# Empty bytes between on-chip buffers, so that streamed activations and weights begin at chosen offsets modulo 256

## The chip, the cores and the metric

One core of a Trainium2 chip runs the whole program in one launch. The metric is device time in microseconds, the median of several executions. TensorE (PE) multiplies, VectorE (DVE), ScalarE (ACT) and GpSimd (POOL) work beside it, SyncE (SP) issues the loads of weights.

## The reference, cut to what matters

Two networks run one after the other on 256 tokens of 1,024 features. The first has four layers, each a mixer (RWKV-7 in layers 0 and 3, stick-breaking attention in 1, sparse attention "dsa" in 2) and a SwiGLU FFN with 2,816 inner columns. The second has two layers on two token streams (`x` and a context `ctx`, 256 tokens each): FFN, a mixing of four branches with differential attention, FFN; the last layer needs only keys and values of the context.

```
x = x + mixer_i(rms_norm(x));  x = x + swiglu(rms_norm(x), w_gu[i], w_down[i])     # i = 0..3
x = x + 0.5*g * swiglu(mod_norm(x), ffn1);  x = x + g' * mix(mod_norm(x), mod_norm(ctx))
x = x + 0.5*g'' * swiglu(mod_norm(x), ffn2)                                        # and ctx alike
```

All is fp32. Almost all of the work is `h @ w` with 256 tokens and weights that come from HBM once, so eleven FFNs stand at the centre.

## The kernel before, in words

**The product.** An fp32 product is made of three fp32r products (`mm3`, L183 to L187): each operand is split into a first part (hi, the value rounded to fp32r by ACT) and a second part (lo, the rest, by DVE), and hi·hi (L185), hi weight·lo activation (L186) and lo weight·hi activation (L187) are added up in PSUM. The stationary operand is a 128x128 piece of a weight's part; the moving operand is 128 features x 256 tokens of an activation's part, 256 columns. In the page's names `whi`, `wlo` are the weight's parts, `hh`, `hl` the parts of a normed activation, `acth`, `actl` those of the FFN's inner activation, `xm` those of rwkv's mixed inputs, `mgh`, `mgl` those of the merged branches.

**Weights.** `wload` (L168) loads 1,024 columns raw (SP's queue) and splits them in pieces of 512 columns: ACT writes `whi`, DVE writes `wlo`, 2,048 bytes per partition each, three buffers of each in the stream's pool. In six FFNs of the main stream (EXTRA: a1, a2, a3, 100, 200, 110; the label is which FFN, layer, stream) two more pairs lie in the FFN's own pool: of every five pieces three use the main buffers and two the extra ones.

**Two streams.** The main stream's pools grow from the low end of SBUF ("left"); a second stream F, with its own weight pool on the right side, does the context's FFNs and mixing beside the main stream wherever the scheduler finds room; its place in the order of work comes from priorities (`spread`, `on`). All engines run their instructions in order, each in its own queue; POOL's queue holds the norms' sums (`norm_scale`, L260), the roots (`rsqrt`, L247), some adds of the mixing and the masks.

**Where buffers lie.** A pool is a stack: tiles lie behind each other by size, in the order of their first use, and pools of a phase are opened and closed again over the same bytes. Sizes per partition: raw weights 4,096, a weight's part 2,048, `hh` or `hl` 8,192, `acth` or `actl` 8,192 (main: 8 blocks) or 5,120 (F: 5 blocks), scratch tiles 1,024: all multiples of 256, so that every buffer's start modulo 256 is that of its pool, set by the small tiles (`const`, tables, vectors) ahead of it. The constants end at 34,528, which is 224 modulo 256; the main weight pool follows (first parts from 46,816, second from 52,960), then the norm's scratch, and the phases' pools start at 62,240, which is 32. The right stack ends at 229,344 (224) and grows downward. That gives, modulo 256:

| where | activations begin at | weight parts, first / second |
|---|---|---|
| main FFNs, mixing, stick-breaking attention | 32 | 224 / 224 |
| the same six FFNs' extra buffers (two pieces in five) | 32 | 32 / 32 |
| dsa, projections | 96 | 224 / 224 |
| rwkv, mixed inputs `xm` | 160 | 224 / 224 |
| F's FFNs: `hh`, `hl` | 160 | 224 / 224 |
| F's FFNs: `acth`, `actl`; F's mixing | 224 | 224 / 224 |

Lines that the change touches: `Kern.__init__` (L71), `wload` (L168), `ffn` (L296), the pools of `rwkv` (L425), `dsa` (L825) and `mixing` (L1094).

Of the kernel before, what the change touches and what calls it, by code (L numbers as in the profile page):

```python
# [8 lines left out]
F32 = mybir.dt.float32  # L9
# [7 lines left out]
P = 128  # L17
# [32 lines left out]
class Packed:  # L50


    def __init__(self):
        self.at, self.n, self.parts = {}, 0, []

    def add(self, name, cols, make):
        self.at[name] = (self.n, cols)
        self.parts.append(make)
        self.n += cols


class Stream:


    def __init__(self, name, wp, side, raw, conv, parts, banks, order=None):
        self.name, self.wp, self.side, self.raw, self.conv, self.parts = name, wp, side, raw, conv, parts
        self.norm = None
        self.banks, self.order, self.turn, self.pace, self.later, self.more, self.count = banks, order, {}, None, None, None, 0


class Kern:  # L71
    def __init__(self, ctx, tc, a, cols):
        self.ctx, self.tc, self.nc, self.a, self.cols = ctx, tc, tc.nc, a, cols
        self.const = ctx.enter_context(tc.tile_pool(name="const", bufs=1))
        wm = ctx.enter_context(tc.tile_pool(name="wm", bufs=1, reuse_waits="tile"))
        self.main = Stream("m", wm, "left", raw=3, conv=3, parts=3,
                           banks={"mm": (0, 1, 2), "sc": (3, 4, 5), "r0": (0, 2, 4), "r1": (1, 3, 5)})
        self.S = self.main
        self.main.norm = ctx.enter_context(tc.tile_pool(name="nm", bufs=1, reuse_waits="tile"))
        self.pp = ctx.enter_context(tc.tile_pool(name="pp", bufs=1, space=PSUM))  # L80
        self.dram = ctx.enter_context(tc.tile_pool(name="dram", bufs=1, space=bass.MemoryType.DRAM))
        self.n = 0
        self.setup()

    def uid(self, s):
# [27 lines left out]
    def vec(self, name, i=0, n=1):  # L113
        at, _ = self.cols.at[name]
        return self.pv[:, at + i : at + i + n]

    def ps(self, tag="mm"):

        S = self.S
        b = S.banks[tag]  # L120
        i = S.turn.get(tag, 0)
        S.turn[tag] = i + 1
        b = b[i % len(b)]
        return self.pp.tile([P, 512], F32, name=self.uid(tag), tag=f"b{b}", bufs=1)
# [43 lines left out]
    def wload(self, src, n):  # L168

        nc, S = self.nc, self.S  # L170
        raw = self.raw(src, n)
        for c in range(0, n, CONV):
            e = min(CONV, n - c)
            self.paced()
            pool, bufs = S.more if S.more and S.count % (S.conv + S.more[1]) >= S.conv else (S.wp, S.conv)
            S.count += 1
            hi = pool.tile([P, CONV], F32R, name=self.uid("whi"), tag="whi", bufs=bufs)
            lo = pool.tile([P, CONV], F32R, name=self.uid("wlo"), tag="wlo", bufs=bufs)
            i = nc.scalar.activation(hi[:, :e], raw[:, c : c + e], AF.Copy)  # L179
            nc.vector.tensor_tensor(lo[:, :e], raw[:, c : c + e], hi[:, :e].bitcast(F32), op=ALU.subtract)  # L180
            yield c, e, hi, lo
# [114 lines left out]
    def ffn(self, pool, hs, w_gu, w_down, add, label):  # L296

        nc = self.nc
        S = self.S
        n = -(-KF // S.parts)  # L300
        S.more = (pool, EXTRA[label]) if label in EXTRA else None
        ends = [KF * (i + 1) // self.S.parts for i in range(self.S.parts)]
        for j0, j1 in zip([0] + ends, ends):
            acts = self.pair(pool, n, "act")[: j1 - j0]
            for j in range(j0, j1):
                p = self.ps()
                self.lin(p[:, :T], w_gu[j, 0], hs)
                self.lin(p[:, T:], w_gu[j, 1], hs)
                t = pool.tile([P, T], F32, name=self.uid("ft"), tag="ns", bufs=2)
                nc.scalar.activation(t, p[:, :T], AF.Tanh, scale=0.5)  # L310
                nc.vector.scalar_tensor_tensor(t, t, 1.0, p[:, :T], op0=ALU.add, op1=ALU.mult)  # L311
                nc.vector.scalar_tensor_tensor(t, t, 0.5, p[:, T:], op0=ALU.mult, op1=ALU.mult)  # L312
                self.split(pool, t, *acts[j - j0])
            for j in range(KD):
                p = self.ps()
                self.lin(p[:, :T], w_down[j][:, j0 * P : j1 * P], acts)
                add(j, p[:, :T])
        S.more = None

    def add_to(self, x):  # L320
# [16 lines left out]
    def rwkv_consts(self):  # L337
# [16 lines left out]
        self.lev = []  # L354
        with self.tc.tile_pool(name="lv", bufs=1, reuse_waits="tile") as A:
            row = A.tile([P, 1], I32, name="lrow")
            col = A.tile([P, HD], I32, name="lcol")
            for h in range(2):
# [3 lines left out]
            for sh in range(6):  # L362

                x = c.tile([P, HD], I32, name=f"lx{sh}")
                y = A.tile([P, HD], I32, name=f"ly{sh}", tag="ly")
                nc.vector.tensor_tensor(x, rowb, col, op=ALU.bitwise_xor)
# [36 lines left out]
    def rwkv(self, i, j, x, front, rear):  # L403

        nc, tc, a = self.nc, self.tc, self.a
        self.rwkv_consts()
        start = tc.cur_priority
        with tc.tile_pool(name=f"rw{j}", bufs=1, reuse_waits="tile") as R:
# [6 lines left out]
            with ExitStack() as es:  # L415
# [7 lines left out]
                    nc.vector.tensor_scalar(dd[:, k, 0:1], h[:, k, 0:1], -1.0, None, op0=ALU.mult)  # L423

                A = es.enter_context(tc.tile_pool(name=f"rwa{j}", bufs=1, reuse_waits="tile"))  # L425

                def plain(m):
                    xs = []
                    for k in range(KD):
                        xs.append(A.tile([P, T], F32, name=self.uid("xp"), tag="xp", bufs=10))  # L430
                        nc.vector.scalar_tensor_tensor(xs[k], dd[:, k], self.vec("rw_mix", (j * 6 + m) * KD + k), h[:, k],
                                                       op0=ALU.mult, op1=ALU.add)
                    return xs

                def first(out, src, xs, rank):
                    w = A.tile([P, KD * P], F32, name=self.uid("w1"), tag="w1", bufs=W1[j])
                    nc.sync.dma_start(w[:, : KD * rank], src)
                    for k, x in enumerate(xs):
                        nc.tensor.matmul(out, w[:, k * rank : (k + 1) * rank], x, start=k == 0, stop=k == KD - 1)
# [99 lines left out]
            with rear as go, tc.tile_pool(name=f"rwc{j}", bufs=1, reuse_waits="tile") as C, self.banks(**RB):  # L539
                ys, base, n, top = [], tc.cur_priority, 0, 0  # L540
                for f in range(KD):
# [3 lines left out]
                    n, top = n or tc.cur_priority - base, max(top, tc.cur_priority)  # L545
# [261 lines left out]
    def dsa(self, i, j, x):  # L807
        nc, tc, a = self.nc, self.tc, self.a
        V = nc.vector
        W3 = T + P  # L810
        with tc.tile_pool(name=f"ds{j}", bufs=1, reuse_waits="tile") as R:
# [11 lines left out]
            wi = R.tile([P, 2, 8], F32, name=self.uid("wi"))  # L823
            os = []
            with tc.tile_pool(name=f"dsa{j}", bufs=1, reuse_waits="tile") as A:  # L825
                hs = self.pair(A, KD, "h")
                self.normed(A, x, lambda f: self.vec("norm_mix", i * KD + f), hs)

                for f in range(5):
                    p = self.ps()  # L830
                    self.lin(p[:, :T], a["ds_w_idx"][j][f], hs)
                    s = A.tile([P, T], F32, name=self.uid("xs"), tag="xs", bufs=2)
# [3 lines left out]
                for tt in range(2):  # L836
                    p = self.ps()
                    for f in range(KD):
                        s = slice(f * 8, (f + 1) * 8)
# [30 lines left out]
                for dst, at, g in ((q, 0, gq), (k, KD, self.vec("ds_k_norm", j))):  # L870
                    for f in range(KD):
                        s = A.tile([P, T], F32, name=self.uid("qs"), tag="qs", bufs=2)
# [13 lines left out]
            with tc.tile_pool(name=f"dsc{j}", bufs=1, reuse_waits="tile") as C:  # L886
                for h in range(16):
# [9 lines left out]
                    s = C.tile([P, 2], F32, name=self.uid("s"), tag="s", bufs=3)  # L897
# [196 lines left out]
    def mixing(self, l, s, x, m, ahead=None):  # L1094

        nc, tc, a = self.nc, self.tc, self.a
# [3 lines left out]
        def sub(name):  # L1100
            return tc.tile_pool(name=f"{name}{l}{s}", bufs=1, reuse_waits="tile")
        with ExitStack() as ahead_pools, sub("mx") as M:
            hs = self.pair(M, KD, "h")
            oc, od, ob, oa = self.pair(M, 4, "oc"), self.pair(M, 2, "od"), self.pair(M, 2, "ob"), self.pair(M, 2, "oa")
            with sub("mn") as N:
                self.mod_norm(N, x, m, s, 1, hs)
            if ahead is not None:
# [379 lines left out]
```

## Time and profile before

| | |
|---|---|
| median of 3 executions | 3950.63 us (3942.87 to 3956.42) |
| the profiled execution | 3951.83 us, span 3950.1 us |
| granted TensorE clock, mean | 0.988 of 2.4 GHz |
| busy | PE 97%, DVE 68%, ACT 52%, POOL 7% |
| bytes read from HBM | 664.84 MB, 170 GB/s over the span |

The span runs from the first to the last instruction. Matmuls overlap in the records: one takes some 0.28 us from start to end, and the next starts when its own weights are in place and the array takes columns, so the spacing from start to start is what a matmul costs in a full stream. The timeline gives starts with two decimals, so spacings are taken over many matmuls. By stage (us in the span): rwkv of layer 0 to 560, its FFN a0 to 810, stick-breaking attention to 960, FFN a1 to 1180, dsa to 1490, FFN a2 to 1710, rwkv of layer 3 to 2250, FFN a3 to 2450, the second network's FFN 100 to 2670, mixing of layer 0 to 3080, FFN 200 to 3270, FFN 110 to 3480, mixing of layer 1 to 3765, FFN 210 to the end. F's FFNs and mixing run between 120 and 810, 920 and 1710, and 1710 and 3080, between the main stream's matmuls.

### The profile page before, as it was taken

The numbers are of one execution on the slowest core, as the hardware profiler recorded it, in microseconds if no ns is written. First come the engines' busy times: TensorE is split into PE (matmuls) and PEld (weight loads), VectorE is DVE, ScalarE is ACT, GpSimd is POOL, SyncE is SP. The second block draws the span as 40 slices with busy tenths as digits, with TensorE's granted clock in tenths as the row PEclk, the third lists the DMA queues.
The fourth block names the chain that finished last, engine by engine and source line by source line (L and its number), as shares of the span: only waits on it lengthen the run. The fifth ranks groups of instructions, "written<-read, shape, count | busy, mean of one in ns | idle before, by whom it ended". The sixth has DMA issues, their size and how long they took to land. (4 is left out here: it accounts for less than half of the span.)

```text
span 3950.1 us, 87281 instructions
## 1 busy us (share of the span) xinstructions
PE 3848.3 (97%) x34750; PEld 3600.8 (91%) x34750; DVE 2693.8 (68%) x5644; ACT 2041.9 (52%) x4137; POOL 295.0 (7%) x333
## 2 busy tenths in 40 slices
PE   7999999998999999999999999999999999999898
PEld 5787999986999999989778999999999999989898
DVE  6355667655777777677556767677966766668766
ACT  3333455577655555545333555555555555555454
POOL 0000000004301110000000100000001000000100
PEclk9999999998999999999999999999999999999999
DMA  7555355642664446646763565664455666644455
GB/s 264 177 168 174 96 170 183 202 148 86 183 183 126 154 155 195 190 128 189 256 227 109 164 187 179 197 186 149 145 181 179 185 190 209 187 146 133 135 180 162
DMA packets 199912, 676.80 MB, mean 171 GB/s; under 512 B 22416, under 2 KB 34960, under 8 KB 199376
## 3 DMA queue, kind: packets, MB, share of 16 engines
q1 hardware_dynamic: 196912, 668.66, 54.3%
q8 instruction: 273, 4.47, 0.5%
q10 hardware_dynamic: 2592, 2.56, 0.2%
q14 instruction: 135, 1.11, 0.1%
HBM read 664.84 MB, written 6.29 MB: 170 GB/s over the span
## 5 line engine op out<-in xcount | busy, mean ns | idle before, releaser
L180 DVE TENSOR_TENSOR wlo<-wraw,whi 128x512 fp32r<-128x512 f32 (+3 forms) x2256 | 1533.2, 687 | 854.0 <-ACT whi L179 810.8
L179 ACT ACTIVATE whi<-wraw 128x512 fp32r<-128x512 f32 (+3 forms) x2256 | 1370.9, 615 | 1349.8 <-PE mm L186 1117.3
L185 PE MATMUL mm<-hh,whi 128*128 128x256 f32 x5496 | 1542.0, 283 | 13.0 <-ACT hh L282 9.0
L187 PE MATMUL mm<-hh,wlo 128*128 128x256 f32 x5496 | 1543.1, 283 | 0.7 <-DVE wlo L180 0.7
L186 PE MATMUL mm<-hl,whi 128*128 128x256 f32 x5496 | 1541.3, 282 | 1.7 <-DVE hl L239 1.1
L185 PEld LDWEIGHTS mm<-hh,whi 128*128 128x128 f32 x5496 | 1039.2, 190 | 31.7 <-ACT hh L282 10.9
L186 PEld LDWEIGHTS mm<-hl,whi 128*128 128x128 f32 x5496 | 1039.6, 190 | 21.8 <-issue 13.4
L187 PEld LDWEIGHTS mm<-hh,wlo 128*128 128x128 f32 x5496 | 1038.4, 190 | 20.7 <-issue 13.9
L185 PE MATMUL mm<-acth,whi 128*128 128x256 f32 x1936 | 537.7, 282 | 3.5 <-DVE ft L312 1.2
L186 PE MATMUL mm<-actl,whi 128*128 128x256 f32 x1936 | 540.7, 282 | 0.4 <-DVE actl L239 0.4
L187 PE MATMUL mm<-acth,wlo 128*128 128x256 f32 x1936 | 538.6, 282 | 0.3 <-DVE wlo L180 0.3
L185 PEld LDWEIGHTS mm<-acth,whi 128*128 128x128 f32 x1936 | 363.2, 189 | 11.7 <-issue 5.3
L186 PEld LDWEIGHTS mm<-actl,whi 128*128 128x128 f32 x1936 | 365.0, 189 | 5.7 <-issue 4.1
L187 PEld LDWEIGHTS mm<-acth,wlo 128*128 128x128 f32 x1936 | 363.8, 189 | 5.5 <-issue 3.0
L260 POOL TENSOR_TENSOR nacc<-nacc,nsq 128x256 f32<-128x256 f32 x114 | 95.4, 838 | 1714.8 <-ACT nsq L259 1713.8
L247 POOL TENSOR_TENSOR ry<-ry,mhalf 128x4 f32<-128x4 f32 (+2 forms) x77 | 82.8, 1076 | 1477.7 <-DVE ry L246 1411.7
L238 ACT ACTIVATE acth<-ft 128x256 fp32r<-128x256 f32 x242 | 100.6, 416 | 55.9 <-DVE ft L312 48.9
L951 PE MATMUL mm<-wada,c 128*32 128x384 f32 x768 | 105.3, 522 | 11.3 <-DMA wada<-in_w_ada 11.3
L239 DVE TENSOR_TENSOR actl<-ft,acth 128x256 fp32r<-128x256 f32 x242 | 104.1, 430 | 4.0 <-ACT acth L238 3.2
L312 DVE SCALAR_TENSOR_TENSOR ft<-ft,mm 128x256 f32<-128x256 f32 x242 | 101.4, 419 | 6.4
L311 DVE SCALAR_TENSOR_TENSOR ft<-ft,mm 128x256 f32<-128x256 f32 x242 | 100.2, 414 | 0.0
L185 PE MATMUL mm<-xm,whi 128*128 128x256 f32 (+1 forms) x328 | 92.8, 287 | 1.9 <-ACT L L481 1.0
(433 smaller groups left out, 4838.4 us busy)
## 6 DMA issues: line engine op xcount, KB each, us to landing
wraw<-in_ffn_w_gu SPq DMA_DIRECT2D x484, 512.0 KB, 4.0
wada<-in_w_ada SPq DMA_DIRECT2D x96, 768.0 KB, 4.5
wraw<-in_w_g SPq DMA_DIRECT2D x96, 512.0 KB, 3.6
wraw<-in_ffn_w_down SPq DMA_DIRECT2D x64, 448.0 KB, 3.4
wraw<-in_ffn_w SPq DMA_DIRECT2D x64, 448.0 KB, 3.4
wraw<-in_rw_w_rkv SPq DMA_DIRECT2D x48, 512.0 KB, 3.9
wraw<-in_ffn_w SPq DMA_DIRECT2D x72, 256.0 KB, 2.8
wraw<-in_ffn_w_down SPq DMA_DIRECT2D x32, 512.0 KB, 3.6
```

What stands on the lines that cost most here:

```text
L179: i = nc.scalar.activation(hi[:, :e], raw[:, c : c + e], AF.Copy)
L180: nc.vector.tensor_tensor(lo[:, :e], raw[:, c : c + e], hi[:, :e].bitcast(F32), op=ALU.subtract)
L185: t.matmul(out, w[0], x[0], start=first, stop=False)
L186: t.matmul(out, w[0], x[1], start=False, stop=False)
L187: t.matmul(out, w[1], x[0], start=False, stop=last)
L238: self.nc.scalar.activation(hi, x, AF.Copy)
L239: self.nc.vector.tensor_tensor(lo, x, hi.bitcast(F32), op=ALU.subtract)
L247: nc.gpsimd.tensor_tensor(y, y, self.mhalf[:, :n], op=ALU.pow)
L260: (nc.vector if k in fast else nc.gpsimd).tensor_tensor(acc, acc, sq, op=ALU.add)
L311: nc.vector.scalar_tensor_tensor(t, t, 1.0, p[:, :T], op0=ALU.add, op1=ALU.mult)
L312: nc.vector.scalar_tensor_tensor(t, t, 0.5, p[:, T:], op0=ALU.mult, op1=ALU.mult)
L951: nc.tensor.matmul(p[32 * i : 32 * (i + 1), :384], c[:, k], raw[:, 384 * i : 384 * (i + 1)], start=k == 0, stop=k == KD - 1)
```

## The change

A method `gap` writes zeros on POOL to a tile that nothing reads, 64 to 192 bytes per partition, and so moves all that lies behind it. It is called at eight places: behind the main weight pool (128 bytes), between first and second parts in each weight pool at its first use (128: the main pool, F's pool, the extra buffers' pools), in the FFNs of EXTRA behind the first inner activations (64), in F's FFNs ahead of the inner activations (192) and at the end (64), at the head of the pools for rwkv's mixed inputs (128) and for dsa (192), and in F's mixing (64). No other instruction is touched.

```diff
+        self.n = 0
+        self.gap(ctx.enter_context(tc.tile_pool(name="sp", bufs=1)), 128)
         self.main.norm = ctx.enter_context(tc.tile_pool(name="nm", bufs=1, reuse_waits="tile"))
...
+    def gap(self, pool, n, tag="gap"):
+
+        self.nc.gpsimd.memset(pool.tile([P, n // 4], F32, name=self.uid(tag), tag=tag), 0.0)
...
             hi = pool.tile([P, CONV], F32R, name=self.uid("whi"), tag="whi", bufs=bufs)
+            if pool not in S.seen:
+                S.seen.append(pool)
+                self.gap(pool, 128, "mid")
             lo = pool.tile([P, CONV], F32R, name=self.uid("wlo"), tag="wlo", bufs=bufs)
...
+        if S.norm is None:
+            self.gap(pool, 192)
         for j0, j1 in zip([0] + ends, ends):
             acts = self.pair(pool, n, "act")[: j1 - j0]
+            if S.more and j0 == 0:
+                self.gap(pool, 64)
...
+        if S.norm is None:
+            self.gap(pool, 64, "end")
         S.more = None
...
                 A = es.enter_context(tc.tile_pool(name=f"rwa{j}", bufs=1, reuse_waits="tile"))
+                self.gap(A, 128)
...
             with tc.tile_pool(name=f"dsa{j}", bufs=1, reuse_waits="tile") as A:
+                self.gap(A, 192)
...
             oc, od, ob, oa = self.pair(M, 4, "oc"), self.pair(M, 2, "od"), self.pair(M, 2, "ob"), self.pair(M, 2, "oa")
+            if s:
+                self.gap(M, 64)
```

`S.norm` is set for the main stream only, so the two gaps that ask for it lie in F's FFNs.

## Rows read from the trace of the kernel before

**Rows 1.** Summary of the page: span, then busy time of each engine.

```profile
span 3950.1 us, 87281 instructions
...
PE 3848.3 (97%) x34750; PEld 3600.8 (91%) x34750; DVE 2693.8 (68%) x5644; ACT 2041.9 (52%) x4137; POOL 295.0 (7%) x333
```

**Rows 2.** The chain that ended last: shares of the span by line.

```profile
PE mm L187 6%; PE mm L186 6%; PE mm L185 6%; DVE wlo L180 0%; PE sc L213 0%; PE mm L231 0%; PE mm L233 0%; PE mm L232 0%; PE mm L1038 0%; DMA wraw<-in_w_qk 0%; DVE hl L283 0%; DVE mgl L1158 0%; DMA wraw<-in_w_br 0%; DVE gt L1153 0%; DVE nh L277 0%
```

**Rows 3.** Page's costliest groups: streamed matmuls on normed activations and inner ones.

```profile
L185 PE MATMUL mm<-hh,whi 128*128 128x256 f32 x5496 | 1542.0, 283 | 13.0 <-ACT hh L282 9.0
...
L185 PE MATMUL mm<-acth,whi 128*128 128x256 f32 x1936 | 537.7, 282 | 3.5 <-DVE ft L312 1.2
```

**Rows 4.** Timeline of PE, FFN 110 (EXTRA): start us, duration us, matmul.

```profile
3304.43 0.28 PE L185 MATMUL mm<-hh,whi 128*128 128x256 f32 x1
3304.55 0.28 PE L186 MATMUL mm<-hl,whi 128*128 128x256 f32 x1
...
3304.91 0.28 PE L186 MATMUL mm<-hl,whi 128*128 128x256 f32 x1
3305.02 0.28 PE L187 MATMUL mm<-hh,wlo 128*128 128x256 f32 x1
...
3308.87 0.28 PE L185 MATMUL mm<-hh,whi 128*128 128x256 f32 x1
3308.99 0.28 PE L186 MATMUL mm<-hl,whi 128*128 128x256 f32 x1
3309.11 0.28 PE L187 MATMUL mm<-hh,wlo 128*128 128x256 f32 x1
```

**Rows 5.** Timeline of PE, F's mixing, activation and weight at 224.

```profile
1379.26 0.28 PE L187 MATMUL mm<-hh,wlo 128*128 128x256 f32 x1
...
1380.94 0.28 PE L186 MATMUL mm<-hl,whi 128*128 128x256 f32 x1
```

**Rows 6.** Timeline of PE, dsa, activation at 96, weight at 224.

```profile
1255.60 0.27 PE L185 MATMUL mm<-hh,whi 128*128 128x256 f32 x1
...
1257.14 0.28 PE L186 MATMUL mm<-hl,whi 128*128 128x256 f32 x1
```

**Rows 7.** Timeline of PE, FFN 210 (no EXTRA), activation 32, weight 224.

```profile
3817.78 0.28 PE L185 MATMUL mm<-hh,whi 128*128 128x256 f32 x1
...
3838.04 0.28 PE L186 MATMUL mm<-hl,whi 128*128 128x256 f32 x1
```

**Rows 8.** Timeline of PE, rwkv 1 beside F's FFN, activations 160, weights 224.

```profile
1831.78 0.28 PE L185 MATMUL mm<-hh,whi 128*128 128x256 f32 x1
...
1833.59 0.28 PE L185 MATMUL mm<-hh,whi 128*128 128x256 f32 x1
1833.71 0.28 PE L186 MATMUL mm<-xm,whi 128*128 128x256 f32 x1
...
1835.97 0.28 PE L185 MATMUL mm<-hh,whi 128*128 128x256 f32 x1
```

**Rows 9.** Groups of PE in 3822 to 3844, then in 3305.9 to 3308.6.

```profile
L186 PE MATMUL mm<-hl,whi 128*128 128x256 f32 x63 | 17.6, 280 | 0.0
L187 PE MATMUL mm<-hh,wlo 128*128 128x256 f32 x63 | 17.6, 279 | 0.0
...
L187 PE MATMUL mm<-hh,wlo 128*128 128x256 f32 x9 | 2.5, 276 | 0.0
```

**Rows 10.** Windows: length, PE busy (count), weight loads, DVE, ACT, POOL, clock.

```profile
2260.00:2650.00 390.00, 390.00 (x3349) 389.91 (x3348) 267.58 (x500) 214.40 (x402) 9.83 (x12) 1.00 0.63 189
1510.00:1690.00 180.00, 180.00 (x1548) 180.00 (x1547) 119.50 (x223) 98.89 (x184) 7.18 (x8) 1.00 0.63 190
3090.00:3270.00 180.00, 180.00 (x1551) 180.00 (x1550) 123.44 (x227) 100.19 (x188) 4.76 (x6) 1.00 0.63 189
```

**Rows 11.** Window of the last mixing, same columns.

```profile
3480.00:3765.00 285.00, 273.05 (x2077) 255.70 (x2076) 215.05 (x439) 145.84 (x289) 20.47 (x18) 0.98 0.45 140
```

**Rows 12.** Groups of POOL over the span: count, busy us, mean ns, idle before.

```profile
L260 POOL TENSOR_TENSOR nacc<-nacc,nsq 128x256 f32<-128x256 f32 x114 | 95.4, 838 | 1714.8 <-ACT nsq L259 1713.8
L247 POOL TENSOR_TENSOR ry<-ry,mhalf 128x4 f32<-128x4 f32 (+2 forms) x77 | 82.8, 1076 | 1477.7 <-DVE ry L246 1411.7 <-ACT whi L179 66.0
...
L1479 POOL MEMSET const-float32-1.0<- 128x1 f32 x1 | 0.1, 99 | 0.0
```

More of the change, by code (lines that the diff above doesn't have):

```diff
@@ L66, in __init__ @@
         self.name, self.wp, self.side, self.raw, self.conv, self.parts = name, wp, side, raw, conv, parts
-        self.norm = None
+        self.norm, self.seen = None, []
         self.banks, self.order, self.turn, self.pace, self.later, self.more, self.count = banks, order, {}, None, None, None, 0
@@ L81, in __init__ @@
         self.dram = ctx.enter_context(tc.tile_pool(name="dram", bufs=1, space=bass.MemoryType.DRAM))
-        self.n = 0
         self.setup()
```

## The prediction

> **What bounds the kernel now.** I read the page's summary first: PE is busy for 97% of the span, nothing else for more than 68% [rows 1]. Then the chain of waits: the three lines of the streamed product, L185 to L187, carry 6.2% each, more than anything else on it [rows 2]. The engine therefore waits for little; the question is how fast its matmuls follow each other. The page's list of groups gives their number: 5,496 triples on the normed activations and 1,936 on the FFN's inner ones [rows 3], 22,296 matmuls; the code adds 3,048 of the same form (mixed inputs, attention outputs, merged branches), so 25,344 of the page's 34,750. One FFN is 22·2·8·3 + 22·8·3 = 1,584 of them.
>
> Then I laid the timeline beside the addresses of the section on the layout, and formed the distance of weight start minus activation start, modulo 256. Every matmul below streams 256 columns against a 128-column weight, at full granted clock, with no wait ahead of it:
>
> - Distance 0, both at 32: from 3304.43 to 3304.91 the starts lie 0.48/4 = 120 ns apart [rows 4]. Distance 0, both at 224: from 1379.26 to 1380.94 in 14 steps, 120.0 ns [rows 5].
> - Distance 128 (activation 96, weight 224): 1255.60 to 1257.14 in 13 steps, 118.5 ns [rows 6].
> - Distance 192 (activation 32, weight 224): two answers. Right behind the block at 120 ns in rows 4, from 3304.91 to 3308.87 in 35 steps, 113.1 ns (113.3 with the rounding of starts); in the last FFN, from 3817.78 to 3838.04 in 172 steps, 117.8 ns [rows 7].
> - Distance 64 (activation 160, weight 224): 1831.78 to 1835.97 in 37 steps, 113.2 ns [rows 8].
>
> So there are three paces, 113.3, 117.8 and 120 ns, and the form of the instruction is the same in all. Which one holds goes with the distance, and at 192 also with what ran before. The duration that the profile gives a matmul repeats it: 280 and 279 ns in the last FFN, 276 within the fast stretch of rows 4 [rows 9].
>
> **The change, part by part.** *Where buffers begin.* By adding up tile sizes: 128 bytes behind the main weight pool plus 128 between its parts shift all behind it by 256, so the main activations stay at 32, the first parts at 224, and the second parts go from 224 to 96. Distances in a triple become 192, 192, 64 (they were 192 three times). In the six FFNs with extra weight buffers (EXTRA: a1, a2, a3, 100, 200, 110) 64 + 128 bytes put the extra pair at 96 and 224 instead of 32 and 32: distances 64, 64, 192 instead of 0. The right stack grows downward, so 128 bytes between its parts put F's first parts at 96 and its second at 224; 192 + 64 in the FFN's pool and 64 in the mixing bring its activations from 160 and 224 to 32: distances 64, 64, 192 instead of 64 or 0. The gaps of 128 and 192 in the rwkv and dsa pools bring xm and hh from 160 and 96 to 32. No matmul at distance 0 or 128 is left.
>
> *What the present paces cost above 113.3 ns.* (1) Six FFNs with EXTRA, 9,504 matmuls: three windows in which PE ran little else give 390.00/3349 = 116.4, 180.00/1548 = 116.3 and 180.00/1551 = 116.1 ns [rows 10], say 116.3: two weights in five at 120, the rest near 113.3. 9,504 · 3.0 = 28 us. (2) The FFNs a0 and 210, without EXTRA, 3,168 matmuls at 117.8 [rows 7]: 3,168 · 4.5 = 14 us. (3) The other 12,672 (F's FFNs, mixings, projections) have no clean window; their blocks lie at 113.2, 117.8, 118.5 and 120 [rows 5 to 8], and I take the mean of those four, 117.4, less a little for the many at 113: 117.0, so 12,672 · 3.7 = 47 us (ends: 30 at 115.7, 57 at 117.8). Sum 89 us, with ends 72 and 99.
>
> *What of it comes out.* The new triple, 192, 192, 64, stands nowhere in the trace, so its pace is the unknown. Bounds by the nearest rows: 113.3 at one end, as both 192 and 64 run there [rows 4, 8]; at the other 117.8 [rows 7]. Lower than 113.3 I exclude, since no stretch of such matmuls shows it; 120 too, since it goes with distance 0 alone. I take 113.3: in rows 4 a stretch at 192 takes it up without any change in its own addresses and keeps it for 35 matmuls, up to the next block at 120; in rows 8 two streams interleave at 64 and hold it; the fast order survives in either, so a triple made of both has a pace that both sides keep, while each slow order belongs to one distance. A step from 192 to 64 in every triple is a small push out of that slow order, as the 120 block is in rows 4. But each wait on weights or a norm starts the sequence afresh, and a little of the saved time will be spent in waits: PE is less than fully busy in the attention stages, for instance 273.05 of 285 us [rows 11]. I count 80% of the sum: 71 us.
>
> *What it adds.* 25 small fills on POOL (2 at set-up, 12 in the six EXTRA pools, 7 for F's weights and FFNs, 4 in rwkv, dsa and mixing). The nearest rows are POOL's set-up fills of 99 ns [rows 12], together 2.5 us on an engine that is idle for 93%. Their price lies in POOL's queue: a fill waits until the memory it covers is free, and behind it stand the norm's sums (L260, 838 ns, 114 of them) and the roots (L247, 1,076 ns) [rows 12], for which the phase's first activations, and so its first matmuls, wait. Ends: 0, where POOL was idle anyway (L260 alone was preceded by 1,714 us of idleness), and one sum late per norm, 114/6 = 19 norms with six sums each on POOL, 19 · 0.84 = 16 us. I take 1, nearest to the idle end, since the norms' sums wait for ACT's squares. The same tiles in new places bring no other instruction, no transfer and no wait; the loads have no new trigger except PE's own faster release of weight buffers. If PE runs 2% faster, ACT and DVE must prepare weights 2% faster: DVE, at 68%, has the room, and would be late next only at phase starts.
>
> Sum: 3951.8 of the profiled execution (span 3950.1) − 71 + 1 = 3882. The profiled execution lies 1.2 us above the median shown, 3950.6, so I give 3882 against that median too.
>
> **The rivals.** (a) *Half the gain.* The fast order is taken up in the triples but lost at each break, or only a part of the stretches finds it. For it: the last FFN keeps 117.8 for 172 matmuls without slipping over [rows 7]. 89/2 = 44, less the waits: 3911.
>
> (b) *Slower: the slow order everywhere.* In the EXTRA FFNs the fast order follows a block at distance 0 [rows 4], while FFNs without such blocks run at 117.8 [rows 7]. If it is the 120 ns block that resets the order, the change removes what it was good for: 9,504 · (117.8 − 116.3) = +14 us; F's projections at 64 and the interleaved xm, some 4,150 matmuls with perhaps half at 113.2 [rows 8], +9; F's inner activations and mixing at 224, about 3,000 at 120 [rows 5], −7. Together +16: 3967. It decides where more than nine in ten of all matmuls run at 117.8: break-even with the mean of 116.8 is (117.8 − 116.8)/4.5 = 22% at the fast pace, and 0.3% slower is reached below 12%. Against it: rows 8, where distance 64 is fast without any such block.
>
> (c) *Nothing happens.* The pace hangs on another thing that goes with the stage (buffer turns, other engines' traffic), and addresses are only its companion: 3951. Against it: rows 4 switch from 120 to 113 and back within one stage and one code path, where only the weight buffer changes. The Trainium skill, "SBUF — State Buffer", section "Who interferes with whom", speaks for this rival: PE reads streamed operand and weights through two independent ports and waits on no one, so starts modulo 256 could not matter. By that rule the sum would be 0 to +2; the three paces in one stage speak against it.
>
> (d) *The roles are swapped.* In EXTRA pools and on F's side the first parts come to 96, not 224 as the change's words say. With all distances still 64 or 192 the time stays that of the forecast, or of (a) if only the order 192, 192, 64 is good.
>
> **How the numbers follow.** Forecast (with d) 0.62; (a) 0.13; (c) 0.10; (b) 0.15. No change of under 0.3%, about 12 us, can be told from none by a measurement of this kernel. Faster takes the forecast and (a), less a little of (a)'s edge, 0.74; same is (c) and that edge, 0.12; slower is 0.14. The range starts at 3951 − 89 = 3862, a little lower for the upper end of (3): 3858; it reaches to 3955, over (a) and half of (c), and leaves out (b) and little else.
>
> **What would show it.** Right: in the last FFN's timeline starts 113.3 ns apart instead of 117.8 and a mean duration of 276 instead of 280; the window 2260 to 2650 shorter by some 10 us for the same 3,349 matmuls; no block at 120 in an EXTRA FFN. Wrong: 117.8 in most windows means (b); blocks at 120 with distances of 64 or 192 mean (c); fast main stages and slow F stages mean that the roles in (d) count; a POOL fill ahead of L260 with PE idle at a phase start means that the fills cost more than 1 us.

## The result, and the profile after

The changed kernel takes 3890.82 us, the median of four runs (3878.99 to 3895.20), against 3953.53 us before beside it: a ratio of 0.9846 with an interval of 0.9830 to 0.9862, some 61 us less by the ratio. Two later sets gave 3894.58 and 3890.19 us. Two executions in them had a lower mean granted clock, 3944.53 us at 0.94 and 5353.16 us at 0.651: the first is in the second set's ratio below and widens its interval, the second is in no number here. The profiled execution, 3878.99 us, is the shortest of the four, so its trace shows a little more gain than the median.

The page's first lines, and of its costliest groups the two that answer to [rows 1, 3] (the lines have moved by eight, so L193 to L195 are the triple):

```profile
span 3877.2 us, 87308 instructions
...
PE 3773.0 (97%) x34750; PEld 3529.2 (91%) x34750; DVE 2687.3 (69%) x5644; ACT 2040.4 (53%) x4137; POOL 297.6 (8%) x358
...
L193 PE MATMUL mm<-hh,whi 128*128 128x256 f32 x5496 | 1529.3, 281 | 11.7 <-ACT hh L290 7.6
...
L193 PE MATMUL mm<-acth,whi 128*128 128x256 f32 x1936 | 532.0, 279 | 4.0 <-DVE xc L986 1.5
```

The bound is where it was: PE at 97% of a shorter span, the same number of matmuls. Taken matmul by matmul, the two traces have the very same order of all 34,750. The profiled gain of 73 us is spread over the whole span; at the same place in that order the new trace is 3 us ahead at 238 us of the old one, 20 at 1128, 35 at 1940, 49 at 2786, 65 at 3404 and 71 at 3850. It is the pace; PE's idle time, span less busy, is 104.2 us where it was 101.8. The timeline of the last FFN, the counterpart of [rows 7] (start, duration, engine, line, tile):

```profile
3800.02 0.28 PE L194 MATMUL mm<-hl,whi 128*128 128x256 f32 x1
3800.13 0.28 PE L195 MATMUL mm<-hh,wlo 128*128 128x256 f32 x1
...
3820.08 0.28 PE L194 MATMUL mm<-hl,whi 128*128 128x256 f32 x1
```

From 3800.02 to 3820.08 stand 177 steps, 113.3 ns each, where before every step took 117.8. But the same FFN has a stretch ahead of it that is not fast:

```profile
3732.89 0.28 PE L193 MATMUL mm<-acth,whi 128*128 128x256 f32 x1
3733.00 0.28 PE L194 MATMUL mm<-actl,whi 128*128 128x256 f32 x1
...
3752.50 0.28 PE L193 MATMUL mm<-hh,whi 128*128 128x256 f32 x1
```

19.61 us for 165 steps are 118.8 ns. That is a slow order of the new triple, and slower than the old one. It sets in behind a step of 181 ns at 3724.5, and the fast order is back at 3783.4 with no pause between them:

```profile
3724.51 0.34 PE L195 MATMUL mm<-acth,wlo 128*128 128x256 f32 x1
3724.69 0.28 PE L193 MATMUL mm<-acth,whi 128*128 128x256 f32 x1
...
3783.05 0.28 PE L195 MATMUL mm<-acth,wlo 128*128 128x256 f32 x1
3783.17 0.40 PE L193 MATMUL mm<-acth,whi 128*128 128x256 f32 x2
3783.41 0.28 PE L194 MATMUL mm<-actl,whi 128*128 128x256 f32 x1
```

It ends behind two L193 in a row (x2), a place where the program leaves the order of the triple; the three longest such stretches of the second trace end at places of this kind as well. Whether that is what ends them was not tried; another such place, at 3726.94, ends nothing.

By windows (length, PE busy and count, weight loads, DVE, ACT, POOL, granted clock, DMA share, GB/s), first two of before, an FFN with extra buffers and the last one:

```profile
3100.00:3200.00 100.00, 100.00 (x861) 100.00 (x860) 66.85 (x123) 53.48 (x99) 0.00 (x0) 1.00 0.63 187
3800.00:3860.00 60.00, 60.00 (x512) 60.00 (x511) 40.57 (x74) 31.80 (x60) 0.00 (x0) 1.00 0.62 186
```

and then of the changed kernel, the first line answering to [rows 10]:

```profile
2225.00:2595.00 370.00, 369.98 (x3262) 369.70 (x3261) 261.21 (x491) 209.51 (x394) 7.77 (x11) 1.00 0.63 194
3100.00:3200.00 100.00, 100.00 (x885) 100.00 (x884) 69.25 (x126) 56.58 (x106) 4.00 (x5) 1.00 0.64 195
3735.00:3785.00 50.00, 50.00 (x423) 50.00 (x422) 32.70 (x60) 26.96 (x51) 0.00 (x0) 1.00 0.60 184
3800.00:3860.00 60.00, 60.00 (x532) 60.00 (x531) 41.52 (x75) 35.50 (x67) 3.48 (x5) 1.00 0.61 184
```

A window counts the two or three matmuls that began ahead of it as well, 0.28 us at some 0.115 us each, so I take 2.4 off each count: 100 us hold 858.6 before and 882.6 after, 116.5 and 113.3 ns; the last FFN goes from 117.7 to 113.3 in the fast part, 118.9 in the slow one. The 370 us at 2225 hold 3259.6 matmuls, 113.5 ns each, where [rows 10] gave 116.4.

The starts of all consecutive streamed matmuls of 256 columns at full granted clock, with no other matmul between them, some 24,100 per trace, give the next table. "Fast steps" are those under 115.5 ns, "excess" is the sum of what each step takes beyond 113.33 ns, and a "stretch" below is a run of at least six such steps between two breaks. A break is a step of 140 ns or more, another matmul, or a change of the granted clock, and a stretch has found the fast order at the first of three fast steps in a row. The last column is the ratio to the runs of before on the same chip.

| kernel | distances in a triple | mean step, ns | fast steps | excess, us | ratio to before (interval) |
|---|---|---|---|---|---|
| before | 192,192,192 (main); 0; 64; 128 | 116.99 | 32% | 88 | 1 |
| the change | 192,192,64 and 64,64,192 | 114.14 | 86% | 20 | 0.9846 (0.9830 to 0.9862) |
| the change again | the same | 114.34 | 82% | 24 | 0.9885 (0.9848 to 0.9921) |
| e1, all at 192 | 192,192,192 | 117.27 | 12% | 95 | 1.0036 (1.0023 to 1.0049) |
| e2, all at 64 | 64,64,64 | 114.89 | 66% | 38 | 0.9880 (0.9858 to 0.9902) |
| e3, roles exchanged | 64,64,192 | 113.83 | 91% | 12 | 0.9836 (0.9823 to 0.9849) |
| e5, extra buffers at 192 | as before, without 0 in six FFNs | 117.43 | 15% | 99 | 1.0036 (1.0023 to 1.0049) |
| e7, all 32 bytes further | as the change | 114.23 | 84% | 22 | 0.9849 (0.9833 to 0.9864) |
| e8, gaps without fills | as the change | 114.27 | 83% | 23 | 0.9866 (0.9848 to 0.9884) |
| e10, e3 without fills | 64,64,192 | 113.82 | 92% | 12 | 0.9819 (0.9804 to 0.9833) |

The excess fell by 69 us in the profiled run and 64 in the second one, and their spans are 73 and 57 us shorter than before's: the pace is nearly the whole gain. The profiled executions differ in the granted clock, too: 93 us of the span lie at 1.2 GHz before, 76 and 91 in these two.

### The profile page after: what moved, and what is told of

Its sections match the earlier page's. It is cut to its first block, busy times and chain, and to the rows that moved or that the text cites. A ratio compares the mean times of both kernels' runs of the same rounds, so it can differ in the third digit from the quotient of the medians.

```text
span 3877.2 us, 87308 instructions
## 1 busy us (share of the span) xinstructions
PE 3773.0 (97%) x34750; PEld 3529.2 (91%) x34750; DVE 2687.3 (69%) x5644; ACT 2040.4 (53%) x4137; POOL 297.6 (8%) x358
## 5 line engine op out<-in xcount | busy, mean ns | idle before, releaser
L193 PE MATMUL mm<-hh,whi 128*128 128x256 f32 x5496 | 1529.3, 281 | 11.7 <-ACT hh L290 7.6
L195 PE MATMUL mm<-hh,wlo 128*128 128x256 f32 x5496 | 1531.5, 281 | 1.4 <-DVE wlo L188 1.3
L193 PEld LDWEIGHTS mm<-hh,whi 128*128 128x128 f32 x5496 | 1034.7, 189 | 30.8 <-ACT hh L290 9.8
L195 PEld LDWEIGHTS mm<-hh,wlo 128*128 128x128 f32 x5496 | 1034.3, 189 | 21.9 <-issue 13.6
L193 PE MATMUL mm<-acth,whi 128*128 128x256 f32 x1936 | 532.0, 279 | 4.0 <-DVE xc L986 1.5
L195 PE MATMUL mm<-acth,wlo 128*128 128x256 f32 x1936 | 532.5, 279 | 0.4 <-DVE wlo L188 0.4
L193 PEld LDWEIGHTS mm<-acth,whi 128*128 128x128 f32 x1936 | 360.7, 188 | 12.5 <-issue 5.5
L195 PEld LDWEIGHTS mm<-acth,wlo 128*128 128x128 f32 x1936 | 361.5, 188 | 5.7 <-issue 3.0
L193 PE MATMUL mm<-xm,whi 128*128 128x256 f32 (+1 forms) x328 | 92.7, 287 | 2.7 <-ACT L L496 1.7
```

The lines of the kernel that those rows point to most:

```text
L193: t.matmul(out, w[0], x[0], start=first, stop=False)
L195: t.matmul(out, w[1], x[0], start=False, stop=last)
```

## The experiments

**e1: one distance, 192, everywhere.** No gap between the parts, the lost bytes put elsewhere, the extra buffers at 224:

```diff
-            if pool not in S.seen:
-                S.seen.append(pool)
-                self.gap(pool, 128, "mid")
...
-        self.gap(ctx.enter_context(tc.tile_pool(name="sp", bufs=1)), 128)
+        self.gap(ctx.enter_context(tc.tile_pool(name="sp", bufs=1)), 256)
...
-                self.gap(pool, 64)
+                self.gap(pool, 192)
...
+        self.gap(right("s2"), 128)
```

> All streamed activations still begin at 32 and every weight part, first and second, at 224: each of the three products of a triple stands at distance 192, none at 0 or 128, and the gaps' fills are all there but those between the parts. Theory 'mixed triple' (a triple that holds both 64 and 192 is what leaves the slow order): without the mixture a stretch that starts slowly stays at 117.8 ns, nine in ten matmuls at that pace, mean about 117.3 ns, so 3965 us (3940 to 3975), ratio to before 0.997 to 1.005, and no gain is left. Theory 'no 0 and no 128' (the gain comes from leaving those distances alone): the time of the change, 3890 us, ratio 0.985, mean pace about 114.

Measured: 3961.01 us beside 3948.00, ratio 1.0036: slower than before, with all distances 0 and 128 gone. The windows of FFN 200 and of the last FFN:

```profile
3100.00:3200.00 100.00, 100.00 (x851) 100.00 (x850) 67.97 (x129) 54.30 (x103) 0.00 (x0) 1.00 0.59 183
3800.00:3860.00 60.00, 60.00 (x512) 60.00 (x510) 40.38 (x74) 31.92 (x59) 0.00 (x0) 1.00 0.61 186
```

60/509.6 = 117.7 ns and 100/848.6 = 117.8: the slow order throughout both windows, and 88% of all steps are slow. "No 0 and no 128" falls; the first theory's time and pace hold.

**e2: one distance, 64, everywhere.** As e1, with 128 bytes ahead of both weight pools, so that all parts lie at 96 (the extra buffers' gap stays at 64):

```diff
-            if pool not in S.seen:
-                S.seen.append(pool)
-                self.gap(pool, 128, "mid")
...
+        self.n = 0
+        self.gap(ctx.enter_context(tc.tile_pool(name="s0", bufs=1)), 128)
         wm = ctx.enter_context(tc.tile_pool(name="wm", bufs=1, reuse_waits="tile"))
...
+        self.gap(right("s2"), 128)
         F = Stream("f", right("wf"), "right", raw=3, conv=3, parts=5,
```

> As before, but every weight part, first and second, at 96: all three products at distance 64. Theory 'mixed triple': about seven stretches in ten find the fast pace in the first few matmuls, as the mixed inputs of rwkv did in the kernel before, the rest stay at 117.8 until the next break, mean about 115.2 ns, 3915 us (3900 to 3930), ratio about 0.990. Theory 'no 0 and no 128': 3890 us, ratio 0.985.

Measured: 3898.76 us, ratio 0.988, mean step 114.89: between the two theories in time, a little better than the first had it. The pace shows what it is. FFN 100, then FFN 200:

```profile
2500.00:2600.00 100.00, 100.00 (x852) 100.00 (x851) 66.92 (x124) 54.74 (x102) 0.00 (x0) 1.00 0.60 184
3100.00:3200.00 100.00, 100.00 (x885) 100.00 (x884) 68.75 (x127) 56.83 (x104) 0.00 (x0) 1.00 0.62 194
```

100/849.6 = 117.7 in one and 100/882.6 = 113.3 in the other: the same code at the same distances, all slow or all fast. Of 361 stretches between breaks, 250 found the fast order, half of them within 3 steps and nine in ten within 4; 111 never did, and one of these held the slow order for 1,670 steps. So 64 alone is a throw at each break that falls well in seven of ten and mostly stands to the next break (two stretches left the slow order later, after 344 and 934 steps); 192 alone falls badly in 322 of 351.

**e3: the roles exchanged in the main stream.** The gap of 128 bytes moves from behind the main weight pool to ahead of it; first parts lie at 96 and second ones at 224, as they already do in the extra buffers and in F:

```diff
+        self.n = 0
+        self.gap(ctx.enter_context(tc.tile_pool(name="s0", bufs=1)), 128)
         wm = ctx.enter_context(tc.tile_pool(name="wm", bufs=1, reuse_waits="tile"))
...
-        self.n = 0
-        self.gap(ctx.enter_context(tc.tile_pool(name="sp", bufs=1)), 128)
```

> The change with the roles of the main weight buffers exchanged: first parts at 96, second parts at 224, so that every triple of the kernel stands at 64, 64, 192, and none at 192, 192, 64. Theory 'two steps at 64 in a row end the slow order' (in the changed kernel the stretches that begin with 64, 64, 192 are fast after at most 14 matmuls, those with 192, 192, 64 after up to 495): slow steps fall from some 3,400 to some 1,600, 8 us less than the change, 3882 us (3877 to 3886), ratio to before 0.9825. Theory 'any mixture does': the time of the change, 3890 us, ratio 0.9846.

Measured: 3881.31 us (3879.34 to 3886.76), where the change beside it had 3894.58: 13 us less, ratio to before 0.9836. The windows of FFN 200 and the last FFN:

```profile
3100.00:3200.00 100.00, 100.00 (x885) 100.00 (x884) 69.86 (x127) 57.31 (x108) 2.70 (x4) 1.00 0.63 195
3800.00:3860.00 60.00, 60.00 (x532) 60.00 (x531) 41.31 (x75) 35.29 (x66) 3.20 (x4) 1.00 0.64 192
```

Both at 113.3 ns. Every stretch of more than 13 steps found the fast order, within 12; in the changed kernel one that began with triples 192, 192, 64 took 495 (543 in the second trace), while those of 64, 64, 192 alone took 12. The order of the roles matters.

**The change again**, beside e1 to e3.

> The change once more, beside the three others on one chip, to set them against it: 3890 us, ratio to before 0.983 to 0.986, streamed matmuls at a mean of 114.1 ns, 86% of them at 113.3.

Measured: 3894.58 us, ratio 0.9885 (0.9848 to 0.9921), mean step 114.34, 82% fast. What differs from the first trace is mostly the two FFNs without extra buffers, 115.9 ns instead of 114.4, and of these the last one: 118.2 instead of 115.1, where FFN a0 has 113.6 in both. In this run the last FFN is no faster than before the change (117.8).

**e4: the fills with no shift.** Every gap is 256 bytes, so no start changes modulo 256:

```diff
-                self.gap(pool, 128, "mid")
+                self.gap(pool, 256, "mid")
...
-            self.gap(pool, 192)
+            self.gap(pool, 256)
```

and so at the other six places.

> All 25 fills of the change, each over 256 bytes instead of 64 to 192, so that every start modulo 256 is that of the kernel before; nothing else differs. This is the price of the fills and of what they hold up in POOL's queue. Theory 'the fills are hidden': 3949 us, ratio 0.998 to 1.002. Theory 'the fills hold up the norms' sums': up to 16 us more, ratio 1.002 to 1.004. The paces are those of before in either case (mean 117.0 ns).

Measured: 4050.01 us, ratio 1.0257 (1.0242 to 1.0272). Neither theory had that. The paces are indeed those of before (mean 116.99 ns), so moving the starts by whole 256 bytes changes none, yet 100 us are lost. The order of the matmuls departs from that of before at 1506 us, while the change left it alone. e9 below takes this up.

**e5: only the blocks at distance 0 of the six FFNs removed.** The kernel before, with the extra buffers at 224:

```diff
             acts = self.pair(pool, n, "act")[: j1 - j0]
+            if S.more and j0 == 0:
+                self.gap(pool, 192)
```

> The kernel before with one edit: the extra weight buffers of the six FFNs begin at 224 instead of 32, so that these FFNs stand at distance 192 throughout and have no more blocks at distance 0; all else stays, F's distances among it. Theory 'a block at distance 0 sets the fast order that follows it': the six FFNs go from 116.3 to 117.8 ns, +14 us, 3962 us, ratio 1.0035 (1.002 to 1.005), though each block itself gains 2 ns. Theory 'the block at distance 0 only costs': two weights in five fall from 119.9 to 114 to 118 ns, 7 to 22 us less, ratio 0.9945 to 0.998.

Measured: 3962.11 us, ratio 1.0036 (1.0023 to 1.0049): 13 us slower, as the first theory said. FFN 200:

```profile
3100.00:3200.00 100.00, 100.00 (x851) 100.00 (x850) 66.97 (x124) 52.78 (x98) 0.00 (x0) 1.00 0.60 185
```

100/848.6 = 117.8 ns instead of 116.5. A block at 120 ns is itself slow but puts the matmuls behind it into the fast order. Of the steps at distance 192 in these six FFNs, 79 to 92% are fast before, FFN by FFN, and 0 to 20% in e5.

**e6: other distances.** Each main FFN of the kernel before gets another distance by a gap at the head of its pool:

```diff
+DIST = {"a0": 32, "a1": 96, "a2": 160, "a3": 224, "100": 128, "200": 0, "110": 192, "210": 64}
...
         with self.tc.tile_pool(name=f"ffn{i}", bufs=1, reuse_waits="tile") as pool:
+            self.gap(pool, (192 - DIST[f"a{i}"]) % 256 or 256, "head")
...
+            if s == 0:
+                self.gap(pool, (192 - DIST[f"{which}{l}{s}"]) % 256 or 256, "head")
...
+            if S.more and j0 == 0:
+                self.gap(pool, DIST[label] or 256)
```

> The kernel before with its eight main FFNs at eight distances: all weights stay at 224, and the activations of an FFN (and its extra buffers with them, to keep one distance per FFN) are moved by a gap at the head of its pool: distance 32 in a0, 96 in a1, 160 in a2, 224 in a3, 128 in 100, 0 in 200, 192 in 110, 64 in 210. Theory 'four classes of 64 bytes, by the block in which a start lies': 120 ns at 0 and, as 192 lies in the same block as 224, at 32; 113.3 or 117.8 at 64 and 96; 118.7 at 128 and 160; 117.8 at 192 and 224. Theory 'the distance itself, smoothly': the steps in between have paces in between, for instance 115 to 117 at 96 and 160, and one below 113.3 is possible at 32, 96, 160 or 224. The time is no test of either.

Measured: 3964.17 us in one run. Windows within the FFNs at distance 96, 160, 224, 128, 0, 192 (two) and 64 (two), in this order:

```profile
1100.00:1160.00 60.00, 60.00 (x514) 60.00 (x513) 39.85 (x73) 33.39 (x63) 2.04 (x2) 1.00 0.63 188
1620.00:1680.00 60.00, 60.00 (x502) 60.00 (x501) 39.70 (x73) 32.75 (x61) 2.03 (x2) 1.00 0.60 181
2376.00:2436.00 60.00, 60.00 (x517) 60.00 (x516) 39.95 (x73) 33.65 (x63) 1.57 (x2) 1.00 0.61 190
2590.00:2650.00 60.00, 60.00 (x502) 60.00 (x501) 39.42 (x71) 32.16 (x60) 1.79 (x2) 1.00 0.60 184
3205.00:3265.00 60.00, 60.00 (x503) 60.00 (x502) 39.56 (x72) 32.88 (x61) 1.03 (x1) 1.00 0.58 180
3312.00:3372.00 60.00, 60.00 (x512) 60.00 (x511) 41.27 (x78) 32.24 (x60) 0.00 (x0) 1.00 0.63 193
3415.00:3475.00 60.00, 60.00 (x532) 60.00 (x531) 41.35 (x75) 34.86 (x66) 3.41 (x4) 1.00 0.65 195
3815.00:3860.00 45.00, 45.00 (x399) 45.00 (x399) 31.06 (x57) 25.39 (x47) 0.00 (x0) 1.00 0.67 199
3885.00:3945.00 60.00, 60.00 (x512) 60.00 (x511) 40.46 (x73) 34.34 (x65) 3.20 (x4) 1.00 0.57 177
```

Less 2.4 per count: 96: 117.3 ns; 160: 120.1; 224: 116.6; 128: 120.1; 0: 119.9; 192: 117.7 and 113.3; 64: 113.5 and 117.7. Other parts of FFNs 96, 128 and 224 ran at 118.7, 118.7 and 117.8. At distance 32 F's matmuls cut in every few us; a stretch of it:

```profile
665.16 0.28 PE L192 MATMUL mm<-hh,whi 128*128 128x256 f32 x1
...
666.82 0.28 PE L194 MATMUL mm<-hh,wlo 128*128 128x256 f32 x1
```

1.66 us for 14 steps, 118.6 ns. "Four classes of 64 bytes" falls, as 32 is not at 120 and 96 has no fast order; nor is the change with distance a smooth one, as 96, 128 and 160 have 117 to 120 between two distances that reach 113.3. Of the eight distances in steps of 32 only 64 and 192 have the fast order in this run, and none goes below it.

**e7: everything 32 bytes further.**

```diff
+        self.n = 0
+        self.gap(ctx.enter_context(tc.tile_pool(name="s0", bufs=1)), 32)
         wm = ctx.enter_context(tc.tile_pool(name="wm", bufs=1, reuse_waits="tile"))
...
+        self.gap(right("s2"), 224)
         F = Stream("f", right("wf"), "right", raw=3, conv=3, parts=5,
```

> The change with everything 32 bytes further: activations at 64, first and second weight parts of the main stream at 0 and 128, the others' at 128 and 0; all distances are those of the change, but every start is now a multiple of 64. Theory 'the distance alone counts': 3891 us, ratio 0.985, mean pace 114.1 to 114.4. Theory 'a start in the middle of 64 bytes costs something by itself': a stretch at multiples of 64 falls below 113.3 ns, for instance to the 109.2 ns that 256 columns at 2.4 GHz and 2.5 ns give, up to 100 us less; or the slow order is another one.

Measured: 3889.07 us, ratio 0.9849 (0.9833 to 0.9864), mean step 114.23. FFN 200 and the last FFN:

```profile
3100.00:3200.00 100.00, 100.00 (x884) 100.00 (x884) 69.46 (x129) 57.49 (x108) 1.10 (x2) 1.00 0.62 188
3800.00:3860.00 60.00, 60.00 (x507) 60.00 (x506) 39.97 (x73) 32.27 (x59) 0.00 (x0) 1.00 0.63 192
```

113.3 ns, and 118.9, the slow order of 192, 192, 64 that the changed kernel's trace has as well. With this shift of 32 bytes the distance counts, not where a start lies by itself. The formula in that expectation is one of the Trainium skill, "TensorE: Matmul & The Clock Gate", section "Back-to-back issue gap", for a single matmul without a weight load of its own. No stretch of 24 steps in any run here has a mean below 113.29 ns.

**e8: the change without fills.** The gap's tile is placed and not written:

```diff
-        self.nc.gpsimd.memset(pool.tile([P, n // 4], F32, name=self.uid(tag), tag=tag), 0.0)
+        pool.tile([P, n // 4], F32, name=self.uid(tag), tag=tag)
```

> The change with its gaps kept and its fills left out: each gap is a tile that is placed and never written, so every start is that of the change and POOL has 25 instructions less. This is the price of the fills alone. Theory 'the fills are hidden': the time of the change beside it, within 3 us, 3888 to 3894, ratio to before 0.984 to 0.987. Theory 'they hold up POOL's queue': 5 to 10 us less than the change, since its trace shows one fill that stands 7.5 us behind a matmul of F.

Measured: 3895.58 us (ratio 0.9866, 0.9848 to 0.9884) where the change beside it had 3890.19 (ratio 0.9853, 0.9835 to 0.9870): the intervals overlap, and the run without fills is not the faster one. The fills cost nothing that these runs can tell. Their groups in the changed kernel's trace, on POOL (count, busy us, mean ns, idle before and its cause):

```profile
L120 POOL MEMSET gap<- 128x16 f32 (+2 forms) x14 | 1.7, 122 | 8.5 <-PE mm L195 7.5 <-PE mm L194 0.7 <-POOLq L1497 0.3
L120 POOL MEMSET mid<- 128x32 f32 x8 | 0.9, 123 | 0.0
...
L120 POOL MEMSET end<- 128x16 f32 x3 | 0.3, 111 | 0.0
```

2.9 us in all. One waits 7.5 us for a matmul (L195), and e8 finds nothing that is late for it.

**e9: 256-byte gaps without fills.** e4 with the line of e8.

> The 256-byte gaps of e4, which gave 4050 us, without a fill. Theory 'room': the bytes cost, because a pool of one stream opens only when the other stack has left its place, and the order of the work shifts with it: 4050 us again (4030 to 4060). Theory 'fills': the fills that wait in POOL's queue cost, so 3950 us (3940 to 3960).

Measured: 4047.15 us, ratio 1.0251 (1.0232 to 1.0269): it was the bytes, not the fills. Two windows of before, in rwkv of layer 3 and at the end of the mixing of layer 0:

```profile
1720.00:1900.00 180.00, 179.04 (x1485) 164.18 (x1483) 128.23 (x283) 98.23 (x213) 2.80 (x2) 1.00 0.58 181
2880.00:3060.00 180.00, 180.00 (x1531) 180.00 (x1531) 121.69 (x205) 96.76 (x179) 17.53 (x14) 1.00 0.57 182
```

and the same of e9:

```profile
1720.00:1900.00 180.00, 165.81 (x1506) 133.17 (x1504) 106.17 (x244) 82.27 (x189) 8.81 (x9) 0.93 0.52 172
2880.00:3060.00 180.00, 152.24 (x992) 133.10 (x991) 133.70 (x311) 81.66 (x174) 5.65 (x5) 0.91 0.35 110
```

PE falls from 180.00 to 152.24 us of 180 in the second window, and the count from 1,531 to 992. By the weights that the matmuls read, F has 293 and 333 of them in the two hundreds from 1700 before, and 32 and 116 in e9; it then does 818 and 555 in those from 2700, where it did 353 and 443, and has 90 left for the rest, where it had 393. So F's work, put off beside rwkv, is used up before the attention of the mixing, and PE finds nothing to do in its waits. Not all of the loss is idle time. The page of e9:

```profile
span 4057.5 us, 87385 instructions
...
PE 3891.3 (96%) x34750; PEld 3627.9 (89%) x34750; DVE 2703.9 (67%) x5644; ACT 2051.7 (51%) x4137; POOL 294.0 (7%) x333
```

Of 107 us more span than in [rows 1], 64 are idle time of PE and 43 are busy time, for the same matmuls, with a lower granted clock: 0.93 and 0.91 in the two windows, where it was 1.00, and 0.976 over the span instead of 0.988. That F's pool could not open beside rwkv for want of room is the likely reason; which tiles met wasn't tried.

**e10: e3 without fills.** Both edits above.

> Triples at 64, 64, 192 everywhere (e3) and no fills (e8): 3879 us (3874 to 3884), ratio to before 0.981 to 0.984, if both parts act as before and the fills are nearly free; 3872 to 3876 if the fills cost 5 to 10 us.

Measured: 3879.02 us (3877.05 to 3881.96), ratio 0.9819 (0.9804 to 0.9833), against 3890.19 for the change on the same chip: the fastest of all, 11 us below the change, 13 by the ratios.

**The change a third time**, beside e8 to e10.

> The change on the same chip as e8 and e10: 3892 us (3887 to 3896), ratio to before 0.984 to 0.987.

Measured: 3890.19 us (3889.70 to 3898.00), ratio 0.9853 (0.9835 to 0.9870).

## Why the prediction was right, and where its steps failed

*What bounds the kernel.* Right: the order of matmuls stayed, PE's idle time grew by 2.4 us only, and nearly all that moved the time is the pace. Rival (c) is out: the paces follow the distances that each kernel sets, and e4 and e7 add that moving starts by whole 256 bytes, or all of them together by 32, leaves the paces as they are. The rule that spoke for it, of the Trainium skill, "SBUF — State Buffer", section "Who interferes with whom", tells which engines wait for each other; what (c) drew from it, that starts cannot matter, does not agree with the traces: starts alone move a step from 113.3 to 120.0 ns.

*The three terms.* I had 28, 14 and 47 us above 113.3 ns, 89 in all. By the starts of the matmuls they were 28.4, 13.5 and 46.2, together 88. The third, taken from four short stretches, was the least sure and came out within 1 us.

*80% of it comes out.* 69 of 88 in the profiled run and 64 in the second, 78% and 72%; the forecast of 70 us net was near (some 61 by the ratio). I gave two reasons for the missing fifth. The first, that each wait starts the sequence afresh, is what the traces show: what is missing is still pace, 1.0 us of the first term, 3 to 8 of the second and 15 of the third, and all of it but 0.3 us lies between a break and the fast order, or in stretches that never find it. The second, that saved time is spent in waits, is hardly there: 2.4 us more idle time. The size of a fifth was worked out from no row, and that it came so near is in part luck.

*"Each slow order belongs to one distance", so the mixed triple cannot hold one.* This step failed. The triple 192, 192, 64 has a slow order of its own, 118.8 ns, and kept it for 165 steps in the stretch shown, 495 in all. (That 120 ns goes with distance 0 alone is wrong as well: e6 has it at 160 and at 128. No matmul of the changed kernel stands there.) What the mixture does is make the slow order easy to leave where 64 follows 64: with 64, 64, 192 the fast order comes within 12 steps in e3, and within 13 in e10. In the changed kernel the swap of roles in the extra buffers and in F, which I held to be neutral in (d), does this work for the main stream, too, since pieces at 64, 64, 192 come between: in the FFNs with extra buffers the mean is 113.4 ns, and in a0, which has none but has F beside it, 113.6. The last FFN has neither and stays at 115.1 and, in the second trace, 118.2. e3 brings it to 113.4, which is some 8 of its 13 us (an estimate: 1,584 steps of 4.8 ns less, against the second trace).

*Once fast, always fast.* I argued from rows 4 that the fast order keeps itself. It does in the changed kernel, to the next break: of 20,471 steps from there on in their stretches, 6 were slow. In the kernel before it was 7,693 of 15,172, mostly because blocks at distance 0 ended it: 165 of the 201 places where fast steps gave way to slow ones are at a matmul at distance 0.

*Rival (b).* Its mechanism is real and its price was near: e5 and e1, which take the blocks at distance 0 away and put nothing in their place, are 13 us slower than before (I had +16). It did not decide here since the mixed triple puts something better in their place.

*Rival (a).* Partly so: the fast order is lost at each break, but found again, in a median of 4 steps. Half of the gain was too little.

*The fills.* 1 us, at the idle end of the bounds; e8 finds nothing. What I had not bounded is the price of the bytes: 256-byte gaps cost 100 us (e4, e9). The change's own gaps are small enough to leave the order of the work as it was.

## What to carry to other kernels

Where PE is the bound and each matmul brings its own weights, compare the start-to-start spacing with the offsets of both operands modulo 256 before looking for waits; here some 24,100 steps lost 3.7 ns each, on average, to where their operands began. Choose offsets so that the fast order is reached from any start, not merely possible: 192 alone was slower than what it replaced, 64 alone was a throw, and 64, 64, 192 found it within 13 steps. Keep gaps small: where two stacks share one memory, some hundred bytes more can change the order of the work, here from 1506 us on (e4, e9).

## What the runs showed of the hardware that was not expected

- A stream of equal matmuls at one full clock has several steady paces, and can keep the one that it falls into: at distance 64, 1,670 steps at 117.8 ns and other FFNs at 113.3 to 113.4, with the same code (e2).
- Of eight distances in steps of 32 bytes, two have the fast order: 64 and 192 (e6, one run). At 0 the pace is 120.0, at 160 120.0, at 128 118.7 or 120.0, at 96 117.3 or 118.7, at 32 118.4, at 224 116.7 or 117.8.
- The slow order of 192, 192, 64 repeats after six steps, five of 117 to 119 ns and one of 124 (the changed kernel's starts). Why these orders exist, and what in the memory or the array sets their steps, stays open: no run here looks below the starts of the matmuls.
